# Probability scaling on GpSimd, modulation products pinned behind each convolution, and three operations for the FFN norm's columns

## The chip, the cores and the metric

One core of a Trainium2 chip runs the program. Its engines are TensorE (PE, with its weight loads PEld), VectorE (DVE), ScalarE (ACT), GpSimd (POOL) and SyncE (SP), whose queue issues most DMAs. Each engine works through its own queue in order, and engines meet at semaphores. The metric is the device time of one execution in microseconds (us), lower is better.

## The reference

One layer of a streaming encoder over 1024 tokens of width 1024, all in fp32:

```
mod = silu(c) @ w_ada + b_ada;  sh_m, sc_m, g_m, sh_f, sc_f, g_f = split(mod, 6)
h = rmsnorm(x, norm_mix_w) * (1 + sc_m) + sh_m
z, xbc, dt, q, k, v = split(h @ w_in)
y_ssd = ssd_mixer(z, silu(causal_dwconv4(xbc) + b), dt)     # 8 heads x 64, state 128
y_att = softmax(q k / 8 + bias over own chunk and 8 before) @ v   # 8 heads x 64, chunks of 64
x = x + g_m * (concat(y_ssd, y_att) @ w_out)
h = rmsnorm(x, norm_ffn_w) * (1 + sc_f) + sh_f
x = x + g_f * (silu(g) * val) @ w_down,   g, val = split(causal_dwconv3(h @ w_up))
out = rmsnorm(x)
```

A modulation column is a product of 1024 weights with silu(c) for each of 128 channels; there are 48 of them, eight for each of the six vectors.

## The kernel before

Everything stays on one core. Matrix products split each fp32 operand into a high and a low part (`split`, lines 60 to 66) and run three matmuls (`mm3`, L56 to L58). The stages in order of time are: norm and the first projections; attention by four pairs of heads; eight convolution columns of the SSD mixer; the z projection; the SSD scan; the output projection; the FFN.

**Attention.** For a pair of heads and a row block of 128 queries, `attn_scores` (L296) makes scores in a PSUM tile `s` (two buffers of two banks). L318 on DVE adds the bias and takes the maximum, L321 on ACT takes the exponential and the sum, L323 the reciprocal, and L324 on DVE scales the probabilities `p` by it. `attn_pv` (L328) transposes them on PE (L350, L353), splits the result (ACT L65, DVE L66) and multiplies with v. There are 64 scalings, 32 of them 128x640, the others shorter. `p` has eight buffers. Projections of the later pairs run between the pairs. Their weights are split into high (ACT, L65) and low (POOL, L66, tile `wl`) parts, so do the convolutions' weights. POOL also writes two memsets into each bias tile (L377, L378).

**Convolution columns.** `conv_silu` (L407) loads weights (L128), splits them, runs 48 matmuls into an `s` tile, evicts with a scale on ACT (L412), adds three shifted taps on DVE (L414), and then does tanh on ACT (L419) and a product on DVE (L420) for each half. The `s` tile comes free with the third tap. The order is four columns for B and C (`bt`, `ct`), then four for x (`xst`), whose results are transposed on PE (L492).

**Modulation products.** `mod_col` (L111) loads 512 KB of weights into a tile and multiplies and sums it on DVE (L113) against `rowa`. Behind each of the eight convolutions, `mods` makes three: the mixer gate, the FFN scale and the FFN shift. Their tiles `mt` come from the pool `mtp` with three buffers. `mod_scale` (L168, L170) and `mod_shift` (L174) turn each column into the FFN norm's columns `affn` and `bffn`, which are first read by L805 and L807. The FFN gate's eight products come later, from the tile tag `rm` (L582).

**z projection.** The pool `mtp` is closed at L519, and `wzp`, with the z weights `wzh` and `wzl` (four buffers each) and `zt`, is opened on the same side at L524. Raw weights pass through `raws`, a ring of two. L62 on ACT writes the high part and L63 on DVE the low part; `z_tile` (L537) reads both.

**What sets the order.** The code is written in one program order, and a scheduler places each instruction in its engine's queue by a planned time: among ready instructions the earlier in program order goes first, so a product of a later convolution may stand ahead of an earlier convolution's taps, and matmuls of the convolutions are placed between those of the last pair. `tc.issue_after(i)` keeps the instructions of its block behind `i` on `i`'s engine; it adds no semaphore. A tile's memory comes free when its last reader is done.

Of the kernel before, what the change touches and what calls it, by code (L numbers as in the profile page):

```python
# [13 lines left out]
ALU = mybir.AluOpType  # L14
# [5 lines left out]
KT = D // P  # L20
# [25 lines left out]
def tile_block(ctx: ExitStack, tc: tile.TileContext, x, crep, pk, w_ada, w_first, w_ft, w_z,  # L46
               w_out, w_up, w_down, bias, fnw, out, dbg=None):
    nc = tc.nc
    V, A, G, T = nc.vector, nc.scalar, nc.gpsimd, nc.tensor
# [31 lines left out]
    modc = const.tile([P, 48], F32, name="modc")  # L81
# [25 lines left out]
    def raw_tile(n=1024):  # L107
        rawc[0] += 1
        return raws[:, rawc[0] % 2, 0:n]

    def mod_col(ft, t):  # L111
        nc.sync.dma_start(t, w_ada[ft])
        V.tensor_tensor_reduce(out=t, in0=t, in1=rowa, scale=1.0, scalar=0.0,  # L113
                               op0=ALU.mult, op1=ALU.add, accum_out=modc[:, ft:ft + 1])

    def row_of(cols, dst, psp, tag, bufs, ones, tmp):
        for hh in range(2):
# [45 lines left out]
    affn = const.tile([P, 8], F32, name="affn")  # L163
    bffn = const.tile([P, 8], F32, name="bffn")

    def mod_scale(dst, sc, nw, kt):
        t = stat()
        V.tensor_tensor(t, modc[:, sc + kt:sc + kt + 1], pkt[:, B_ADA + sc + kt:B_ADA + sc + kt + 1],  # L168
                        ALU.add)
        V.scalar_tensor_tensor(dst[:, kt:kt + 1], t, 1.0, pkt[:, nw + kt:nw + kt + 1],  # L170
                               op0=ALU.add, op1=ALU.mult)

    def mod_shift(dst, sh, kt):
        V.tensor_tensor(dst[:, kt:kt + 1], modc[:, sh + kt:sh + kt + 1],  # L174
                        pkt[:, B_ADA + sh + kt:B_ADA + sh + kt + 1], ALU.add)

    V.tensor_scalar(pkt[:, SCW:FCW], pkt[:, SCW:FCW], 0.5, None, op0=ALU.mult)
    V.tensor_scalar(pkt[:, SNW:SCW], pkt[:, SNW:SCW], 512.0 ** 0.5, None, op0=ALU.mult)
# [63 lines left out]
    for hh in range(2):  # L242
        accs = [ps0.tile([P, 512], F32, tag="acc0", bufs=6, name="acc0") for _ in range(6)]
        for kt in range(KT):
            if hh == 0:
# [4 lines left out]
                t = raw_tile(768)  # L250
# [12 lines left out]
            c = slice(hh * 512, hh * 512 + 512)  # L263
# [23 lines left out]
    def s_tile():  # L287
        return ps1.tile([P, 1024], F32, tag="s", bufs=2, name="s")

    def p_tile():  # L290
        return pp.tile([P, 640], F32, tag="p", name="p")

    def tp_tile():
        return ps1.tile([P, 512], F32, tag="tp", bufs=2, name="tp")

    def attn_scores(p, i, bt):  # L296
        d = qk[p]
        j0 = max(0, i - 4)
        n = (i - j0 + 1) * P
        off = (j0 - (i - 4)) * P  # L300
        parts = [(0, n)] if n <= 512 else [(0, 320), (320, 320)]
        st = [s_tile(), s_tile()]
        for h in range(2):
            for pi, (a, w) in enumerate(parts):
                for ti, kn in enumerate(("kh", "kl")):
                    T.matmul(st[h][:, 512 * pi:512 * pi + w], d["q"][h][:, i * P:(i + 1) * P],  # L306
                             d[kn][h][:, j0 * P + a:j0 * P + a + w], start=ti == 0, stop=ti == 1)
        res = []
        for h in range(2):
            pt_ = p_tile()  # L310
            nm, rs = stat(), stat()
            if len(parts) == 1:
                src, bsl, dst = st[h][:, 0:n], bt[h][:, off:off + n], pt_[:, 0:n]
            else:
                src = st[h].rearrange("p (a b) -> p a b", a=2)[:, :, 0:320]
                bsl = bt[h].rearrange("p (a b) -> p a b", a=2)
                dst = pt_.rearrange("p (a b) -> p a b", a=2)
            V.tensor_tensor_reduce(out=dst, in0=src, in1=bsl, scale=-1.0, scalar=3e38,  # L318
                                   op0=ALU.add, op1=ALU.min, accum_out=nm)
            pv_ = pt_[:, 0:n]  # L320
            A.activation(pv_, pv_, AF.Exp, scale=-1.0, bias=nm, accum_out=rs)  # L321
            rr = stat()
            V.reciprocal(rr, rs)  # L323
            V.tensor_scalar(pv_, pv_, rr, None, op0=ALU.mult)  # L324
            res.append(pt_)
        return res

# [79 lines left out]
    def conv_silu(ft, dst, th2):  # L407
        wh, wl = wu_pair(w_ft[ft], A, G)
        ps = s_tile()
        gemm_ft(wh, wl, [ps[:, 0:512], ps[:, 512:1024]], hts_h, hts_l)  # L410
        w = [pkt[:, SCW + 4 * ft + j:SCW + 4 * ft + j + 1] for j in range(4)]
        A.activation(dst, ps, AF.Identity, scale=w[3], bias=pkt[:, SCB + ft:SCB + ft + 1])  # L412
        for j in range(1, 4):
            V.scalar_tensor_tensor(dst[:, j:S], ps[:, 0:S - j], w[3 - j], dst[:, j:S],  # L414
                                   op0=ALU.mult, op1=ALU.add)
        for hh in range(2):
            c = slice(hh * 512, hh * 512 + 512)
            th = th2()
            A.activation(th, dst[:, c], AF.Tanh)  # L419
            V.scalar_tensor_tensor(dst[:, c], th, 1.0, dst[:, c], op0=ALU.add, op1=ALU.mult)  # L420

    part = lambda p, w: (lambda: gemm_part(p, w))
    attention(0)
# [13 lines left out]
    bt_ = [bcx.tile([P, S], F32, name=f"bt{g}") for g in range(2)]  # L437
    ct_ = [bcx.tile([P, S], F32, name=f"ct{g}") for g in range(2)]
# [31 lines left out]
    def mt_tile():  # L470
        return mtp.tile([P, D], F32, tag="mt", bufs=MTB, name="mt")

    def mods(kt):
        mod_col(G_M + kt, mt_tile())
        mod_col(SC_F + kt, mt_tile())
        mod_scale(affn, SC_F, NFFN, kt)
        mod_col(SH_F + kt, mt_tile())
        mod_shift(bffn, SH_F, kt)

    for g in range(2):  # L480
        conv_silu(4 + g, bt_[g], th512)
        mods(2 * g)
        conv_silu(6 + g, ct_[g], th512)
        mods(2 * g + 1)
    for ft in range(4):
        xt = bcp.tile([P, S], F32, tag="rm", bufs=2, name="xst")
        conv_silu(ft, xt, th512)
        mods(4 + ft)
        for hh in range(2):
            tps = tp_tile()  # L490
            for j in range(4):
                T.transpose(tps[:, j * P:(j + 1) * P], xt[:, (4 * hh + j) * P:(4 * hh + j + 1) * P],  # L492
                            ident)
            A.activation(xs[:, 4 * hh:4 * hh + 4, ft * P:(ft + 1) * P],
                         tps.rearrange("p (a b) -> p a b", a=4), AF.Copy)
    wop_ = []
    halves = [slice(0, 512), slice(512, 1024)]
    order = [4, 5, 6, 7, 0, 1, 2, 3]
# [347 lines left out]
    class Unit:  # L846
# [98 lines left out]
    for sts in ((0, 1), (2, 3)):  # L945
        h_raw(sts)
        c = slice(sts[0] * P, sts[-1] * P + P)
# [61 lines left out]
    sc, last_load, busy, queue = [0], [], {}, []  # L1009
# [219 lines left out]
    last = product("P2", W, tail=True)  # L1229
# [63 lines left out]
```

## Time and profile before

| | us |
|---|---|
| median of 3 runs (1269.13 to 1275.05) | 1270.45 |
| the profiled execution | 1271.27 |
| its span, first to last instruction | 1269.6 |
| PE busy | 1189.2 |
| DVE busy | 984.6 |
| ACT busy | 560.4 |
| POOL busy | 108.0 |

A group's row gives line, engine and operation, out<-in, shapes and count, then busy time and mean ns, then idle time before it with what ended it. A row in order of time gives the start in us from the span's start, the length, the instruction, and in brackets the idle time of its engine before it with its releaser. A wait's row gives who waited for whom, the total in us, how often, and the longest. The granted clock is TensorE's, as a share of full speed.

### The profile page before, as it was taken

What the parts mean: (1) busy time and instruction counts of PE and PEld (TensorE: products, weight loads), DVE (VectorE), ACT (ScalarE), POOL (GpSimd) and SP (SyncE); (2) the same over time, 40 slices, a digit from 0 to 9 for tenths busy, and PEclk for the clock granted to TensorE, in tenths of its full rate; (3) what the DMA queues carried; (4) which work ended last, traced back from release to release, by engine and by line L of the source; (5) the groups of instructions that cost most, each with busy time, mean ns of one, the idle gap of its engine ahead of it and who ended that gap; (6) DMA issues with size and microseconds to landing.
All of it is one profiled execution on the core that took longest, in us unless ns stands there. A gap on an engine that the chain in (4) does not pass through costs nothing.

```text
span 1269.6 us, 15525 instructions
## 1 busy us (share of the span) xinstructions
PE 1189.2 (94%) x5786; PEld 991.8 (78%) x5786; DVE 984.6 (78%) x1533; ACT 560.4 (44%) x917; POOL 108.0 (9%) x114
## 2 busy tenths in 40 slices
PE   5898999989979979999889999999999999999995
PEld 3686788778869868888668888888888888888884
DVE  7836666694698886764999988888988879856976
ACT  4525555573324453423744444443444445443443
POOL 1300011101220242220000000000000000000002
PEclk9998899999989989999999999999999999999998
DMA  8712111201564422112213322323322295834433
GB/s 331 258 29 65 38 51 54 62 17 34 183 226 140 166 83 67 54 55 90 69 67 124 119 80 90 110 100 124 119 81 89 79 321 208 303 110 143 158 124 132
DMA packets 57835, 150.85 MB, mean 119 GB/s; under 512 B 5793, under 2 KB 5921, under 8 KB 56353
## 3 DMA queue, kind: packets, MB, share of 16 engines
q1 hardware_dynamic: 50704, 125.49, 29.4%
q10 hardware_dynamic: 7056, 24.38, 4.8%
q8 instruction: 45, 0.74, 0.2%
q14 instruction: 30, 0.24, 0.1%
HBM read 116.56 MB, written 29.10 MB: 115 GB/s over the span
## 4 chain that ended last, share of the span: by engine, by line
PE 76%; DVE 14%; DMA 4%; ACT 3%; issue 2%; POOL 1%; SPq 0%; DVEq 0%; POOLq 0%; ACTq 0%
PE dn L57 5%; PE dn L56 5%; PE dn L58 5%; PE uY L56 5%; PE uY L58 5%; PE uY L57 5%; PE uZ L58 3%; PE uZ L56 3%; PE uZ L57 3%; PE uX L56 3%; PE uX L58 3%; PE uX L57 3%; PE acc L56 3%; PE acc L57 3%; PE acc L58 2%
## 5 line engine op out<-in xcount | busy, mean ns | idle before, releaser
L56 PE MATMUL dn<-w 128*128 128x512 f32 x308 | 111.9, 389 | 0.0
L57 PE MATMUL dn<-w 128*128 128x512 f32 x308 | 111.9, 389 | 0.0
L58 PE MATMUL dn<-w 128*128 128x512 f32 x308 | 103.3, 389 | 0.0
L65 ACT ACTIVATE w<-ya 128x1024 fp32r<-128x1024 f32 (+1 forms) x44 | 41.8, 950 | 95.6 <-PE uY L58 87.1
L764 POOL TENSOR_TENSOR st<-st,mhalf 128x1 f32<-128x1 f32 x16 | 12.4, 777 | 678.2 <-DVE st L763 678.2
L56 PEld LDWEIGHTS dn<-w 128*128 128x128 f32 x308 | 57.8, 188 | 12.1
L57 PEld LDWEIGHTS dn<-w 128*128 128x128 f32 x308 | 57.8, 188 | 12.0
L58 PEld LDWEIGHTS dn<-w 128*128 128x128 f32 x308 | 57.8, 188 | 11.9
L65 ACT ACTIVATE w<-xs 128x1024 fp32r<-128x1024 f32 (+1 forms) x44 | 41.8, 951 | 43.5 <-PE uY L58 37.5
L56 PE MATMUL s<-hth,wh 128*128 128x512 f32 x128 | 51.7, 404 | 8.8 <-DVE st L168 8.0
L66 DVE TENSOR_TENSOR pt<-tp,pt 128x512 fp32r<-128x512 f32 (+2 forms) x72 | 42.0, 595 | 17.7 <-ACT pt L65 17.2
L318 DVE CUSTOM_DVE_ANT_0 p<-s,bias 128x640 f32<-128x640 f32 (+4 forms) x64 | 40.8, 649 | 18.4 <-PE s L306 10.1
L321 ACT ACTIVATE p<-p,st 128x640 f32<-128x640 f32 (+4 forms) x64 | 44.1, 691 | 19.8 <-DVE st L318 18.7
L66 POOL TENSOR_TENSOR wl<-raws,wh 128x1024 fp32r<-128x1024 f32 x14 | 36.5, 2612 | 189.3 <-ACT wh L65 145.9
L906 DVE SCALAR_TENSOR_TENSOR a<-cv,pkt,a 128x1023 f32<-128x1023 f32 (+1 forms) x40 | 51.0, 1276 | 0.1
L57 PE MATMUL s<-htl,wh 128*128 128x512 f32 x128 | 51.0, 398 | 0.0
L58 PE MATMUL s<-hth,wl 128*128 128x512 f32 x128 | 50.9, 398 | 0.0
L66 DVE TENSOR_TENSOR w<-ya,w 128x1024 fp32r<-128x1024 f32 (+1 forms) x44 | 47.7, 1085 | 4.0 <-ACT w L65 4.0
L113 DVE CUSTOM_DVE_ANT_0 mt<-mt,rows 128x1024 f32<-128x1024 f32 x32 | 41.6, 1301 | 10.6 <-DMA mt<-in_w_ada_dram 10.6
L906 DVE SCALAR_TENSOR_TENSOR a<-cg,pkt,a 128x1023 f32<-128x1023 f32 (+1 forms) x40 | 49.6, 1276 | 0.0
L65 ACT ACTIVATE pt<-tp 128x512 fp32r<-128x512 f32 (+2 forms) x72 | 36.3, 523 | 28.8 <-PE tp L350 12.3
L66 DVE TENSOR_TENSOR w<-xs,w 128x1024 fp32r<-128x1024 f32 (+1 forms) x44 | 47.6, 1083 | 0.0
(407 smaller groups left out, 3607.6 us busy)
## 6 DMA issues: line engine op xcount, KB each, us to landing
mt<-in_w_ada_dram SPq DMA_DIRECT2D x32, 512.0 KB, 3.8
gz<-a ACTq DMA_DIRECT2D x10, 1024.0 KB, 5.3
adat<-in_w_ada_dram SPq DMA_DIRECT2D x16, 512.0 KB, 6.5
ya<-in_w_up_dram SPq DMA_DIRECT2D x10, 768.0 KB, 4.0
xs<-in_w_up_dram SPq DMA_DIRECT2D x10, 768.0 KB, 4.1
raws<-in_w_ft_dram SPq DMA_DIRECT2D x14, 512.0 KB, 3.5
gy<-a ACTq DMA_DIRECT2D x10, 512.0 KB, 2.6
qk<-in_x_dram SPq DMA_DIRECT2D x8, 512.0 KB, 6.7
```

The costliest lines, as they stand in the source:

```text
L56: T.matmul(ps, lh, rh, start=start, stop=False, skip_group_check=more)
L57: T.matmul(ps, lh, rl, start=False, stop=False, skip_group_check=more)
L58: T.matmul(ps, ll, rh, start=False, stop=stop, skip_group_check=more)
L65: i = A.activation(hi, src, AF.Copy) if ehi is A else ehi.tensor_copy(hi, src)
L66: return i, elo.tensor_tensor(lo, src, f32(hi), ALU.subtract)
L113: V.tensor_tensor_reduce(out=t, in0=t, in1=rowa, scale=1.0, scalar=0.0, op0=ALU.mult, op1=ALU.add, accum_out=modc[:, ft:ft + 1])
L318: V.tensor_tensor_reduce(out=dst, in0=src, in1=bsl, scale=-1.0, scalar=3e38, op0=ALU.add, op1=ALU.min, accum_out=nm)
L321: A.activation(pv_, pv_, AF.Exp, scale=-1.0, bias=nm, accum_out=rs)
L764: G.tensor_tensor(r, ms, mhalf[:, 0:1], ALU.pow)
L906: V.scalar_tensor_tensor(a[:, j:S], c[:, 0:S - j], w[2 - j], a[:, j:S], op0=ALU.mult, op1=ALU.add)
```

## The change

Three edits. L324 moves from DVE (`V`) to POOL (`G`). `conv_silu` returns its last DVE instruction, and the three products of `mods` are issued behind it on DVE; their loads are not held. The FFN norm's columns are made once, behind the last convolution, for all eight columns at once: two operations for `affn` and one for `bffn` in place of 24 single-column ones.

```
     def mod_col(ft, t, at=None):
         nc.sync.dma_start(t, w_ada[ft])
+        with tc.issue_after(at) if at else ExitStack():
             V.tensor_tensor_reduce(out=t, in0=t, in1=rowa, ...)
...
-    def mod_scale(dst, sc, nw, kt):
+    def mod_scale(dst, sc, nw, kt, n=1):        # mod_shift likewise; columns kt to kt + n
...
-            V.tensor_scalar(pv_, pv_, rr, None, op0=ALU.mult)
+            G.tensor_scalar(pv_, pv_, rr, None, op0=ALU.mult)
...
-            V.scalar_tensor_tensor(dst[:, c], th, 1.0, dst[:, c], op0=ALU.add, op1=ALU.mult)
+            last = V.scalar_tensor_tensor(dst[:, c], th, 1.0, dst[:, c], op0=ALU.add, op1=ALU.mult)
+        return last.ins
...
-    def mods(kt):
-        mod_col(G_M + kt, mt_tile())
-        mod_col(SC_F + kt, mt_tile())
-        mod_scale(affn, SC_F, NFFN, kt)
-        mod_col(SH_F + kt, mt_tile())
-        mod_shift(bffn, SH_F, kt)
+    def mods(kt, at):
+        for m in (G_M, SC_F, SH_F):
+            mod_col(m + kt, mt_tile(), at)
...
-        conv_silu(4 + g, bt_[g], th512)
-        mods(2 * g)
-        conv_silu(6 + g, ct_[g], th512)
-        mods(2 * g + 1)
+        mods(2 * g, conv_silu(4 + g, bt_[g], th512))
+        mods(2 * g + 1, conv_silu(6 + g, ct_[g], th512))
...
-        conv_silu(ft, xt, th512)
-        mods(4 + ft)
+        mods(4 + ft, conv_silu(ft, xt, th512))
...
+    mod_scale(affn, SC_F, NFFN, 0, KT)
+    mod_shift(bffn, SH_F, 0, KT)
```

More of the change, by code (lines that the diff above doesn't have):

```diff
@@ L109, in raw_tile, with mod_col @@
         return raws[:, rawc[0] % 2, 0:n]
-    def mod_col(ft, t):
+    def mod_col(ft, t, at=None):
         nc.sync.dma_start(t, w_ada[ft])
-        V.tensor_tensor_reduce(out=t, in0=t, in1=rowa, scale=1.0, scalar=0.0,
-                               op0=ALU.mult, op1=ALU.add, accum_out=modc[:, ft:ft + 1])
+        with tc.issue_after(at) if at else ExitStack():
+            V.tensor_tensor_reduce(out=t, in0=t, in1=rowa, scale=1.0, scalar=0.0,
+                                   op0=ALU.mult, op1=ALU.add, accum_out=modc[:, ft:ft + 1])
     def row_of(cols, dst, psp, tag, bufs, ones, tmp):
@@ L164, in tile_block, with mod_shift @@
     bffn = const.tile([P, 8], F32, name="bffn")
-    def mod_scale(dst, sc, nw, kt):
-        t = stat()
-        V.tensor_tensor(t, modc[:, sc + kt:sc + kt + 1], pkt[:, B_ADA + sc + kt:B_ADA + sc + kt + 1],
+    def mod_scale(dst, sc, nw, kt, n=1):
+        t = stat(n)
+        V.tensor_tensor(t, modc[:, sc + kt:sc + kt + n], pkt[:, B_ADA + sc + kt:B_ADA + sc + kt + n],
                         ALU.add)
-        V.scalar_tensor_tensor(dst[:, kt:kt + 1], t, 1.0, pkt[:, nw + kt:nw + kt + 1],
+        V.scalar_tensor_tensor(dst[:, kt:kt + n], t, 1.0, pkt[:, nw + kt:nw + kt + n],
                                op0=ALU.add, op1=ALU.mult)
-    def mod_shift(dst, sh, kt):
-        V.tensor_tensor(dst[:, kt:kt + 1], modc[:, sh + kt:sh + kt + 1],
-                        pkt[:, B_ADA + sh + kt:B_ADA + sh + kt + 1], ALU.add)
+    def mod_shift(dst, sh, kt, n=1):
+        V.tensor_tensor(dst[:, kt:kt + n], modc[:, sh + kt:sh + kt + n],
+                        pkt[:, B_ADA + sh + kt:B_ADA + sh + kt + n], ALU.add)
     V.tensor_scalar(pkt[:, SCW:FCW], pkt[:, SCW:FCW], 0.5, None, op0=ALU.mult)
```

## The prediction

> **What bounds the kernel now.** I read the page first, then busy time by stage, then the waits and the order of time around the two stages that the diff touches.
>
> ```profile
> span 1269.6 us, 15525 instructions
> PE 1189.2 (94%) x5786; PEld 991.8 (78%) x5786; DVE 984.6 (78%) x1533; ACT 560.4 (44%) x917; POOL 108.0 (9%) x114
> ```
>
> TensorE (PE) is the bound: busy for 94% of the span. A change can only win by removing time in which PE stands still or runs at a low clock, and lose by adding some. GpSimd (POOL) is 9% busy. The profiled execution took 1271.27 us, 1.67 above its span, and 0.82 above the median of the runs (1270.45). The busy times of the stages concerned follow; the columns are the stretch, its length, PE, PEld, DVE, ACT and POOL busy with their instructions, the granted clock, the DMA share and GB/s.
>
> ```profile
> 118.00:133.00 15.00, 12.32 (x72) 9.51 (x71) 14.88 (x45) 12.79 (x31) 0.00 (x0) 0.99 0.08 22
> 250.00:287.00 37.00, 32.56 (x198) 26.89 (x196) 34.21 (x101) 27.64 (x67) 3.02 (x3) 0.95 0.08 23
> 350.00:360.00 10.00, 3.31 (x8) 2.66 (x9) 10.00 (x15) 1.85 (x3) 2.92 (x1) 0.56 0.60 202
> 395.00:460.00 65.00, 60.56 (x454) 55.91 (x453) 52.10 (x94) 28.78 (x64) 12.31 (x8) 1.00 0.43 147
> ```
>
> VectorE (DVE) is full in two stretches of the attention (118 to 133 and 250 to 287), where PE idles 2.68 and 4.44 us. It is full again in the convolution stage, where PE has one large hole at 350. Its cause, and what it costs, in the waits of PE and in PE's instructions in order of time:
>
> ```profile
> PE s L56 <- DVE st L168: 8.0, 1, 8.0
> ```
> ```profile
> 356.69 0.77 PE L56 MATMUL s<-hth,wh 128*128 128x512 f32 x1 [7.96 <-DVE st L168]
> 357.26 0.63 PE L57 MATMUL s<-htl,wh 128*128 128x512 f32 x1
> 357.69 0.63 PE L58 MATMUL s<-hth,wl 128*128 128x512 f32 x1
> ...
> 361.50 0.40 PE L58 MATMUL s<-hth,wl 128*128 128x512 f32 x1
> 361.74 0.40 PE L56 MATMUL s<-hth,wh 128*128 128x512 f32 x1
> ```
>
> PE waits 7.96 us for a score bank, which the third tap (L414) of the fourth convolution frees. Then 11 matmuls run 0.43 apart instead of 0.23: 11 x 0.20 = 2.2 us. The hole costs 10.2 us. DVE was late because modulation products stood ahead of that tap:
>
> ```profile
> 333.41 1.22 DVE L113 CUSTOM_DVE_ANT_0 mt<-mt,rows 128x1024 f32<-128x1024 f32 x1 [1.94 <-DMA mt<-in_w_ada_dram]
> ...
> 340.14 2.89 DVE L113 CUSTOM_DVE_ANT_0 mt<-mt,rows 128x1024 f32<-128x1024 f32 x1 [0.44 <-DMA mt<-in_w_ada_dram]
> ...
> 354.13 1.21 DVE L113 CUSTOM_DVE_ANT_0 mt<-mt,rows 128x1024 f32<-128x1024 f32 x1
> ...
> 355.28 1.27 DVE L414 SCALAR_TENSOR_TENSOR ct<-s,pkt,ct 128x1021 f32<-128x1021 f32 x1
> ```
> ```profile
> 338.86 3.09 POOL L66 TENSOR_TENSOR wl<-raws,wh 128x1024 fp32r<-128x1024 f32 x1 [2.58 <-ACT wh L65]
> ```
>
> Nine products ran from 333.41 to 354.13. The one at 340.14 took 2.89 instead of 1.22, and began to move when the split on POOL ended (338.86 + 3.09 = 341.95): the two engines block one another when both read two SBUF operands.
>
> **The change, part by part.**
>
> *Scaling (L324) on POOL.* 64 instructions leave DVE; these are the ones in the two full stretches (DVE only), and the nearest rows for a price on POOL:
>
> ```profile
> 118.00:133.00 15.00, 4.45 (x9) 0.99 0.08 22
> 250.00:287.00 37.00, 9.47 (x20) 0.95 0.08 23
> ```
> ```profile
> L66 POOL TENSOR_TENSOR wl<-raws,wh x14: 2378/2398/3503, 54.3 to 371.1; 128x1024 fp32r<-128x1024 f32 x14
> ```
> ```profile
> L96 POOL TENSOR_SCALAR st<-st x16: 221/222/1162, 8.0 to 587.9; 128x1 f32<-128x1 f32 x16
> ```
> ```profile
> PE tp L353 <- DVE p L324: 0.2, 1, 0.2
> ```
>
> DVE gains 4.45 and 9.47 us there, about 0.48 per block. The price of one 128x640 scaling on POOL lies between 0.22 (the fixed cost of the 128x1 row) and 2.40 x 640/1024 = 1.50 (two operands). I take 0.9, the middle, since the operation is that of the first row and the size nearer the second. A block is then 0.4 us later. That is hidden: PE waited for L324 only once, 0.2 us, because the DVE queue itself delayed the scaling. PE cannot win more than it idles: 2.68 + 4.44 = 7.1 us. ACT, 12.79 of 15 busy in the first stretch, is the next limit (15 - 12.79 = 2.2 of the 2.68). The chain through ACT and the in-order queues will take part of the rest. I take half: **-3.5**, ends -7.1 and 0. Without that cover, see the second rival. On POOL's queue the scalings stand among six of the 2.40 us splits and the bias memsets.
>
> The Trainium skill speaks against this gain ("Perfetto Trace Analysis", Optimizing Scalar/DVE Operations): since GpSimd reads through VectorE's second port, moving work between the two might not help. The blocked product at 340.14 agrees where both read SBUF twice. In the attention, L318, L66 and L367 each read one operand from PSUM, so I do not apply it; by it the sum would be 3.5 higher.
>
> *Products pinned.* The three products of a convolution may no longer run before its last L420. Their DMAs are not pinned, but the three mt buffers come free only with the products, so the loads wait too. On SP's queue the loads of the z weights may stand behind them; the product of the seventh convolution frees these before the seam below, so I cost that at nothing. Two places decide.
>
> First, the hole at 350. The attention's last DVE operation is the first row here; the second is one of the small ones that the diff merges:
>
> ```profile
> 335.92 0.42 DVE L367 TENSOR_TENSOR ya<-pv,tl 64x256 f32<-64x256 f32 x1
> ...
> 338.40 0.15 DVE L174 TENSOR_TENSOR bffn<-modc,pkt 128x1 f32<-128x1 f32 x1
> ```
>
> It ends at 336.3, and PE could start the GEMM at 356.69 - 7.96 = 348.7. Rows in order of time overlap their neighbours by about 0.07, so a tap counts 1.2. DVE must do in between: the first convolution's L420 (2 x 0.6), three products (3 x 1.21), the second's L420 (1.2), three products (3.6, if their loads are in time), the third's L420 (1.2), three taps (3 x 1.2), one block by a split (1.7 as at 340.14): 16.1, so 352.4. If the third three also come first, 356.0, nearly as now; if the second three are late, 348.8. I take 352.4: the hole shrinks from 8.0 to 3.7, and half the slow matmuls stay (1.1): 10.2 - 4.8 = **-5.4**, ends -10.2 and 0.
>
> The Trainium skill ("TensorE: Matmul & The Clock Gate", What's actually happening) lets the clock fall to half after about 3.4 us without work and for as long again; the 4.6 us from 356.69 fit it roughly. By it a gap of 3.7 us keeps the full penalty, and the sum would be 1.1 higher.
>
> Second, the seam to the z projection. The pool wzp is opened where the pool mtp was, so the z weights' low parts (wzl) lie on the mt tiles and must wait for the last three products. In the profile before these are early:
>
> ```profile
> 388.13 1.22 DVE L113 CUSTOM_DVE_ANT_0 mt<-mt,rows 128x1024 f32<-128x1024 f32 x1
> ...
> 390.68 1.30 DVE L63 SCALAR_TENSOR_TENSOR wzl<-raws,wzh 128x520 fp32r<-128x520 f32 x2
> ...
> 393.93 1.29 DVE L420 SCALAR_TENSOR_TENSOR xst<-th,xst 128x512 f32<-128x512 f32 x2 [0.76 <-ACT th L419]
> ```
> ```profile
> 393.27 1.16 ACT L419 ACTIVATE th<-xst 128x512 f32<-128x512 f32 x2 [2.36 <-DVE xst L414]
> ...
> 394.86 1.19 ACT L412 ACTIVATE xst<-s,pkt 128x1024 f32<-128x1024 f32 x1
> ```
> ```profile
> 394.15 0.41 PE L56 MATMUL zps<-wzh,hth 128*128 128x260 f32 x2
> ```
>
> The last product ran at 388.13, wzl followed at 390.68, and z began at 394.15, the moment the last convolution's GEMM ended. After the change the last three products stand behind that convolution's L420. From the end of its GEMM: 1.19 (L412) + 3 x 1.2 (L414) + 0.6 (tanh) + 2 x 0.6 (L420) + 3 x 1.21 (products) + 0.65 (wzl) = 10.9 us before PE can go on. PE has the transposes of two x tiles meanwhile, 4 x 0.44:
>
> ```profile
> 397.43 0.44 PE tp L492 x4
> ```
>
> So 10.9 - 1.8 = 9.1 us of new idling, and 2.2 of slow clock as at 356.69: **+11.3**. Ends: +10.1 if two products free enough, +15.5 if PE also waits for the third weight part, whose raw buffer comes free only with the first wzl (2.9 landing, 0.6, 0.65):
>
> ```profile
> raws<-in_w_z_dram SPq DMA_DIRECT2D x8, 260.0 KB, 2.9
> ```
>
> *What lies behind.* The work of that convolution no longer runs beside z, so DVE is freer from 395 to 460, where PE idles 65 - 60.56 = 4.4. I take **-2**, ends -4.4 and 0.
>
> *Norm columns in three operations instead of 24.* 21 small DVE operations go, of 0.15 us (338.40) at most: 3 us. Their readers come at 592, so nothing waits: 0 on the path by itself.
>
> Sum: -3.5 - 5.4 + 11.3 - 2 = +0.4 on 1271.27, and 0.82 below for the median: **1271 us**. All best ends give 1270.5 - 7.1 - 10.2 + 10.1 - 4.4 = 1259; all worst, 1270.5 + 15.5 = 1286.
>
> **Rivals.** *The pin wins outright.* The seam does not open, because the scheduler lets the z weights start on buffers that are free, and the hole goes: 1270.5 - 3.5 - 10.2 = 1257; or only the attention gives all it can, 1270.5 - 7.1 - 10.2 + 11.3 - 2 = 1262. For it: z's first matmul needs only the high part. Against: the order 388.13, 390.68.
>
> *Scalings queue behind splits (slower).* POOL runs in order, and a split of 2.40 us waits for ACT, which waits for PE. If the scalings of a block stand behind each of the six splits in the attention and PE has nothing else, 6 x 2.4 = 14.4 in place of -3.5: 1289. It decides from 1277 on, that is from two and a half splits. Against: PE has projection matmuls to fill with.
>
> *The pin does not clear the first hole (slower).* Nine products are allowed before the tap as now, if loads are early: 1271 + 5.4 + 2 = 1278.
>
> **How the numbers follow.** 0.5% (6.4 us) is about what a measurement of this kernel can tell from no change. Forecast 0.37 (within 0.5%); pin wins 0.25 (faster); queueing 0.18 and the uncleared hole 0.20 (slower). So faster 0.25, same 0.37, slower 0.38. The range 1259 to 1287 reaches from the best ends to near the queueing case; the forecast's own is 1264 to 1277.
>
> **What would show it.** Right: DVE under 12 of 15 in the first stretch with POOL 5 to 10 busy; the wait at 350 under 5 us; a new PE hole of 8 to 11 us before the first zps matmul, released by wzl. Wrong: a PE wait on POOL p L324 of several us, no hole before zps, or a PE wait of 8 us still at the sixth convolution.

## The result, and the profile after

The changed kernel takes 1276.28 us (median of 20 runs, 1273.11 to 1279.09), the kernel before 1269.45 (20 runs, 1266.0 to 1275.05). The ratio is 1.0049, with a 95% interval of 1.0038 to 1.0060: 0.5% slower, some 6.2 us. The forecast was 1271, within 1264 to 1277, and 1259 to 1287 over all its cases. The profiled execution took 1276.49 us, 1.69 above its span; that of before took 1271.27.

The head of the page of the changed kernel, and its group of scalings (busy us, mean ns of one, idle time before it):

```profile
span 1274.8 us, 15617 instructions
...
PE 1187.0 (93%) x5786; PEld 992.2 (78%) x5786; DVE 960.0 (75%) x1448; ACT 560.8 (44%) x917; POOL 199.0 (16%) x178
...
L325 POOL TENSOR_SCALAR p<-p,st 128x640 f32<-128x640 f32 (+4 forms) x64 | 94.1, 1486 | 30.1 <-DVE st L324 26.3
```

VectorE lost 85 instructions (1533 to 1448) and 24.6 us of work, GpSimd gained 91.0 us of work. In the attention, by stretch (columns as in the prediction):

```profile
118.00:133.00 15.00, 12.92 (x65) 10.46 (x65) 9.27 (x28) 8.80 (x21) 14.85 (x11) 0.89 0.14 46
...
250.00:287.00 37.00, 34.81 (x210) 30.39 (x209) 22.05 (x66) 21.70 (x52) 25.20 (x17) 0.94 0.00 1
```

VectorE was full there before; now GpSimd is the full engine of the first stretch, 14.85 of 15. TensorE idles 2.1 and 2.2 us instead of 2.7 and 4.4. Its waits later on (total us, times, longest):

```profile
PE s L56 <- DVE ct L415: 7.5, 1, 7.5
PE tp L488 <- DVE xst L421: 6.5, 1, 6.5
...
PE zps L57 <- DVE wzl L63: 3.1, 1, 3.1
...
PE uY L56 <- DVE cg L882: 3.1, 1, 3.1
```

The first is the old hole, hardly shorter than before (8.0). The next two are the new hole at the seam to z. The last is at the start of the FFN, where the same wait was 1.4 us before, and which the diff does not touch.

To see where time goes over the whole kernel, five instants are read from each trace. Two of the rows of the changed kernel (shortest, median, longest ns, then first and last start) are:

```profile
L368 DVE TENSOR_TENSOR ya<-pv,tl x32: 398/417/419, 117.1 to 327.5; 64x256 f32<-64x256 f32 x32
...
L58 PE MATMUL zps<-wzh,htl x64: 278/281/420, 400.5 to 447.1; 128*128 128x260 f32 x64
```

They are the first and the last attention output (117.1, 327.5), the last z matmul into a `zps` tile (447.1; those into `s` tiles end some 7 us later in both kernels), and, read in the same way, the first matmul of the FFN (uX, 614.6) and the first of its second part (dn, 1051.1). The stretches between them, in us, for all kernels of this study; the letters are those of the experiments below:

| kernel | to first output | attention | convolutions and z | z to FFN | FFN, first part | rest | median, ratio (95% interval) |
|---|---|---|---|---|---|---|---|
| before | 120.0 | 215.9 | 109.3 | 167.3 | 433.1 | 224.0 | 1269.45 |
| changed | 117.1 | 210.4 | 119.6 | 167.5 | 436.5 | 223.7 | 1276.28, 1.0049 (1.0038 to 1.0060) |
| A scaling alone | 117.7 | 209.5 | 110.7 | 168.4 | 434.8 | 223.6 | 1265.16, 0.9960 (0.9943 to 0.9977) |
| B pin alone | 117.9 | 215.6 | 121.0 | 166.6 | 434.9 | 223.7 | 1282.03, 1.0099 (1.0080 to 1.0118) |
| C columns alone | 117.9 | 217.0 | 110.1 | 169.3 | 434.8 | 223.6 | 1274.60, 1.0038 (1.0023 to 1.0052) |
| D pin and columns | 116.4 | 216.5 | 122.5 | 168.3 | 433.2 | 223.6 | 1282.55, 1.0109 (1.0089 to 1.0130) |
| E last three free | 117.8 | 207.5 | 117.3 | 167.4 | 436.4 | 223.7 | 1272.22, 1.0026 (1.0014 to 1.0039) |
| F tiles apart | 118.0 | 207.4 | 105.3 | 170.8 | 434.7 | 223.7 | 1262.36, 0.9948 (0.9930 to 0.9966) |
| G A, tiles apart | 120.7 | 207.8 | 110.2 | 169.1 | 434.7 | 223.7 | 1266.79, 0.9969 (0.9954 to 0.9984) |
| H A, behind the tap | 120.8 | 207.9 | 111.3 | 168.3 | 437.3 | 223.7 | 1269.42, 0.9997 (0.9984 to 1.0010) |
| I F, behind the tap | 119.2 | 207.4 | 103.4 | 172.3 | 434.8 | 223.6 | 1260.24, 0.9917 (0.9895 to 0.9938) |
| J two-tensor scaling | 120.4 | 209.4 | 120.5 | 167.9 | 434.7 | 223.7 | 1277.02, 1.0062 (1.0044 to 1.0081) |
| K I, six early | 126.6 | 208.7 | 101.5 | 169.6 | 433.1 | 223.7 | 1267.93, 0.9988 (0.9977 to 0.9999) |
| L I, six in the attention | 118.9 | 213.1 | 101.8 | 172.9 | 437.5 | 223.6 | 1267.90, 0.9989 (0.9978 to 1.0001) |

Each line is one profiled execution. The first column needs care: no kernel but K and L moves work into it other than the first few scalings, and yet without K it takes 116.4 to 120.8 us. The granted clock up to 118 us is 0.94 in four of the profiled executions (before, G, H and J), and they are those with 120 and more; in the others, K aside, it is 0.96 to 0.99. So differences of up to 3 us in this column go with the clock of the start. That clock does not follow the scaling (0.99 in A, 0.94 in G and H, which scale in the same place); whether the single execution sets it, one trace of each kernel cannot show. From before to the changed kernel: -2.9 here, -5.5 in the attention, +10.3 in the convolutions and z, +0.2, +3.4 in the FFN, -0.3: +5.2, the difference of the spans.

### The profile page after: what moved, and what is told of

Its sections match the earlier page's. It is cut to its first block, busy times and chain, and to the rows that moved or that the text cites. A ratio compares the mean times of both kernels' runs of the same rounds, so it can differ in the third digit from the quotient of the medians.

```text
span 1274.8 us, 15617 instructions
## 1 busy us (share of the span) xinstructions
PE 1187.0 (93%) x5786; PEld 992.2 (78%) x5786; DVE 960.0 (75%) x1448; ACT 560.8 (44%) x917; POOL 199.0 (16%) x178
## 4 chain that ended last, share of the span: by engine, by line
PE 79%; DVE 11%; ACT 4%; DMA 3%; issue 2%; POOL 1%; SPq 0%; DVEq 0%; POOLq 0%; ACTq 0%
PE dn L57 5%; PE dn L56 5%; PE dn L58 5%; PE uY L56 5%; PE uY L58 5%; PE uY L57 5%; PE uZ L56 3%; PE uZ L58 3%; PE uZ L57 3%; PE uX L56 3%; PE uX L57 3%; PE uX L58 3%; PE acc L56 3%; PE acc L57 3%; PE acc L58 3%; PE s L56 2%
## 5 line engine op out<-in xcount | busy, mean ns | idle before, releaser
L325 POOL TENSOR_SCALAR p<-p,st 128x640 f32<-128x640 f32 (+4 forms) x64 | 94.1, 1486 | 30.1 <-DVE st L324 26.3
L322 ACT ACTIVATE p<-p,st 128x640 f32<-128x640 f32 (+4 forms) x64 | 44.1, 690 | 13.1 <-DVE st L319 12.9
```

What stands on the lines that cost most here:

```text
L325: G.tensor_scalar(pv_, pv_, rr, None, op0=ALU.mult)
```

## The experiments

The theory was that the scaling gains, the pin loses at the seam, and the columns are free. The rivals were that a change of order far behind makes the loss, or that GpSimd's queue takes back the gain.

### A to D: the parts alone

A (`e1_scale`), on the kernel before:

```diff
-            V.tensor_scalar(pv_, pv_, rr, None, op0=ALU.mult)
+            G.tensor_scalar(pv_, pv_, rr, None, op0=ALU.mult)
```

> The kernel before with the scaling of the probabilities on GpSimd and nothing else; products unpinned, norm columns as before. Theory (the attention's gain is the scaling's, the loss is the pin's): the last evicted attention output on VectorE comes at about 328 us as in the changed kernel (before 335.9), x1's GEMM starts some 8 us earlier, no 6.5 + 3.1 us wait opens at the transposes of x and the z GEMM, and the time is about 8 us under the kernel before, 1261 to 1264 us. Rival A (the gain is given back at the first convolutions, because GpSimd's splits block the products as they were before the pin too): within 3 us of before. Rival B (the 3.4 us lost at the start of the FFN come from an order that the scaling moves): the wait of uY for cg shows 3 us instead of 1.4, and the time is near 1265.

B (`e2_pin`), the pin alone, with the norm columns one by one as before:

```diff
-        mods(2 * g)
+        mods(2 * g, conv_silu(4 + g, bt_[g], th512))
...
```

> The kernel before with the three products pinned behind each convolution and nothing else. Theory: the attention ends where it did (335.9 us on VectorE), the first hole stays at 7 to 8 us, and the seam opens as in the changed kernel: waits of 6.5 us of the transposes of x and of 3 us of the z GEMM for the low half of its weights. The time is 1277 to 1284 us. Rival A (the pin costs nothing by itself and only the shifted attention made the seam): within 2 us of 1269.5, no wait over 2 us at the seam. Rival B (the 3.4 us at the start of the FFN are the pin's, by the order of VectorE's instructions behind it): uY's wait for cg shows 3 us here.

C (`e3_merge`), the columns alone:

```diff
-        mod_scale(affn, SC_F, NFFN, kt)
-        mod_shift(bffn, SH_F, kt)
...
+    mod_scale(affn, SC_F, NFFN, 0, KT)
+    mod_shift(bffn, SH_F, 0, KT)
```

> The kernel before with the FFN norm's columns in three operations and nothing else. Theory: the columns are off the path, so that 1268 to 1271 us come out, with every wait up to 600 us as before. Rival (the merged columns make cg later and are the cause of the 3.4 us at the start of the FFN): uY's wait for cg grows from 1.4 to about 3 us, and the time is 1272 to 1274 us.

D (`e4_pin_merge`) is the changed kernel with the scaling back on VectorE:

```diff
-            G.tensor_scalar(pv_, pv_, rr, None, op0=ALU.mult)
+            V.tensor_scalar(pv_, pv_, rr, None, op0=ALU.mult)
```

> The changed kernel with the scaling back on VectorE. Theory (effects add): the scaling's gain of about 8 us is gone and the pin's loss stays, so that 1281 to 1286 us come out. Rival A (the queue of GpSimd costs what it gains): the time is that of the changed kernel, 1275 to 1278. Rival B (scaling on GpSimd was itself the loss): faster than the changed kernel, 1268 to 1272.

Measured: A is 0.4% faster than before, B 1.0% slower, C 0.4% slower, D 1.1% slower. Waits of TensorE in A, then in B, then one in C:

```profile
PE s L56 <- DVE st L168: 8.1, 1, 8.1
...
PE uY L56 <- DVE cg L884: 3.0, 1, 3.0
```
```profile
PE tp L491 <- DVE xst L421: 7.8, 1, 7.8
PE s L56 <- DVE ct L415: 7.6, 1, 7.6
...
PE zps L57 <- DVE wzl L63: 3.1, 1, 3.1
```
```profile
PE s L56 <- DVE zs L553: 2.2, 1, 2.2
```

The seam is the pin's: with it, convolutions and z take 119.6 to 122.5 us (changed, B, D), without it 109.3 to 110.7 (before, A, C), and B has both waits of the changed kernel though nothing else was done. The attention's gain is the scaling's: 215.6 to 217.0 us without it, 207.4 to 210.4 with it (L, which puts other work there, aside). B and D came out within the ranges of the theory. A is 1 us above its range, where its rival B put it, and shows that rival's sign, 3.0 us of uY's wait: its FFN takes 1.7 us longer than before, so a part of the gain is lost there. C was expected at no change and lost 4.8 us (0.38% of 1269.5), near what its rival said, and uY's wait is 3.0 there too. But this wait cannot be the cause: in A and C the wait just ahead of it (uZ for its weights) fell from 3.0 to 1.5, so that the two together are 4.5 against 4.4 before. The granted clock accounts for it: over the first 57 us of the FFN it is 0.94 in A and in C and 0.97 before, 0.03 x 57 = 1.7 us. The rest of C's loss is in no one place: against before, +1.1 in the attention, +0.8 in the convolutions and z (with 3.1 us of waits for `zs` in z, 0.3 before), +2.0 between z and the FFN, and -2.1 in the first column. The effects do not add: B and C sum to 17 us and D, which does both, loses 14.

### E to G: what makes the seam

E (`e5_last_free`), the changed kernel with the last three products free:

```diff
-        mods(4 + ft, conv_silu(ft, xt, th512))
+        at = conv_silu(ft, xt, th512)
+        mods(4 + ft, at if ft < 3 else None)
```

> The changed kernel with the three products of the last convolution not pinned. Theory (the seam is the low z weights waiting for memory that the last three products hold, and for their place behind that convolution's last operation): the wait of the z GEMM for the low weights (3.1 us) and the wait of the transposes ahead of it (6.5 us) go, the first hole stays at 7 to 8 us, and the time is 9 to 12 us under the changed kernel, 1264 to 1268 us. Rival (any pinned product moves the seam, since VectorE is simply late by the work that was pinned): the waits shrink by less than half and the time is 1272 to 1276.

F (`e6_mt_apart`), the changed kernel with the pool of the mt tiles kept open until the pool of the z weights closes, so that they share no bytes:

```diff
-    es_m.close()
...
     es_t.close()
+    es_m.close()
```

> The changed kernel with the modulation rows' tiles in memory of their own, so that the z weights share no bytes with them; the pins stay. Theory (the shared memory makes the wait, the pin only makes it late): the seam closes as with the last three products unpinned, 1264 to 1268 us. Rival (the place in VectorE's queue makes it, memory or not): the transposes still wait 4 us or more, and the time is within 3 us of the changed kernel.

G (`e10_free_apart`) is A with F's edit, so nothing is pinned.

> The kernel with the scaling on GpSimd alone (1265.2 us), with the modulation rows' tiles in memory of their own; nothing pinned. It tells what the pin does where the memory no longer makes it wait (against 1262.4 us with the pin, the merged columns and the same memory). Theory (the memory is the whole gain: the z GEMM can start before the last convolutions and fills TensorE): 1259 to 1264 us, the first hole stays at about 8 us, the first z matmul stands before 370 us. Rival (the pin helps once the memory is apart, because the products no longer take VectorE ahead of the taps): 1265 us or more.

Measured: E is 1272.2, where the rival put it, not 1264 to 1268. Its waits between 360 and 400 us:

```profile
PE s L56 <- DVE affn L171: 5.5, 1, 5.5
PE zps L56 <- ACT wzh L62: 1.9, 1, 1.9
```

The hole did not close: 7.4 us are left of 10.8. VectorE's rows in E, from the third pinned product of the convolution before to the split of the low z weights, and then the row with which TensorE goes on:

```profile
380.79 1.22 DVE L114 CUSTOM_DVE_ANT_0 mt<-mt,rows 128x1024 f32<-128x1024 f32 x1
...
383.32 1.23 DVE L114 CUSTOM_DVE_ANT_0 mt<-mt,rows 128x1024 f32<-128x1024 f32 x1 [1.31 <-DMA mt<-in_w_ada_dram]
...
389.51 1.22 DVE L114 CUSTOM_DVE_ANT_0 mt<-mt,rows 128x1024 f32<-128x1024 f32 x1
...
390.65 1.28 DVE L415 SCALAR_TENSOR_TENSOR xst<-s,pkt,xst 128x1021 f32<-128x1021 f32 x1
...
392.00 1.30 DVE L63 SCALAR_TENSOR_TENSOR wzl<-raws,wzh 128x520 fp32r<-128x520 f32 x2
```
```profile
392.08 0.56 PE L56 MATMUL s<-wzh,hth 128*128 128x260 f32 x1 [5.54 <-DVE affn L171]
```

The freed products are late all the same. There are three buffers, and the pinned products of the convolution before hold them until 382: the next load lands at 383.3, and VectorE stands idle for it. Four products follow, the freed ones among them, and now they stand between the taps of the last convolution (the third at 390.65). TensorE resumes at 392.08 with a z matmul that needs no low weights but a score bank, and that bank comes free with this third tap (390.65 + 1.28 = 391.93; the view names a small operation that ends a little later). Only behind the tap come the low weights, on the same bytes; their first matmul follows at 392.75. So the pin reaches one convolution further than the products that it holds, through their buffers. In F the z weights lie elsewhere, and the scheduler places the first split of the low ones early:

```profile
352.68 0.69 DVE L63 SCALAR_TENSOR_TENSOR wzl<-raws,wzh 128x520 fp32r<-128x520 f32 x1
```

and z starts before the convolutions have ended:

```profile
L56 PE MATMUL zps<-wzh,hth x64: 279/284/687, 359.4 to 430.5; 128*128 128x260 f32 x64
```

The waits at the seam are gone and the stage takes 105.3 us instead of 119.6. F is 1262.4, faster than the kernel before by 0.5%, with the pins in it and 1.6 us below the range of its theory: the shared memory makes the wait, as that theory says. G starts z at 362.5, as expected, but is 1266.8, on its rival's side: separate memory alone is worth nothing without the pins, 110.2 us in the stage against 110.7 in A. Without the pin the seam had no hole to close. G also has the columns unmerged, so G against F is not the pin alone, and their intervals meet.

### H and I: what makes the first hole

H (`e9_behind_tap`) is A with six products pinned behind the third tap of the fourth convolution, all others free:

```diff
...
-        mods(2 * g)
...
-        conv_silu(6 + g, ct_[g], th512)
-        mods(2 * g + 1)
+        if g == 0:
+            mods(0)
+        tap = conv_silu(6 + g, ct_[g], th512)
+        mods(2 * g + 1, tap if g else None)
+        if g == 1:
+            mods(2, tap)
```

> The kernel with the scaling on GpSimd alone (1265.2 us), and in it the six products of the third and fourth convolution pinned behind the third tap of the fourth, all others free. In that kernel five products and a blocked small operation stand on VectorE between 336 and 346 us ahead of the tap that frees the score bank. Theory (that queue makes the 8.1 us hole): the hole shrinks to 0 to 3 us, VectorE gets later by as much further on, so that part of it comes back before the z GEMM, and the time is 1257 to 1263. Rival (VectorE is the bound of the whole stage, 78.7 of 90 us busy): the wait only moves to a later place, and the time is within 2 us of 1265.

I (`c1_hole`) is F with nine products pinned there:

```diff
...
-        mods(2 * g, conv_silu(4 + g, bt_[g], th512))
-        mods(2 * g + 1, conv_silu(6 + g, ct_[g], th512))
+        last = conv_silu(4 + g, bt_[g], th512)[0]
+        if g == 0:
+            mods(0, last)
+        tap = conv_silu(6 + g, ct_[g], th512)[1]
+    for kt in (1, 2, 3):
+        mods(kt, tap)
```

> The changed kernel with the tiles in memory of their own (1262.4 us), and the nine products of the second to fourth convolution pinned behind the third tap of the fourth instead of behind their own convolution. Four of the seven products that stood ahead of that tap no longer do. Theory (the queue of VectorE makes the first hole, and the z GEMM, which may start early here, covers what comes later): the wait of 7.5 us falls under 2, and the time is 1251 to 1257 us. Rival (VectorE is the bound of this stage, 84 of 90 us busy, and what is moved behind the tap stalls the next convolutions): the time is 1260 to 1264 us.

Measured: the hole is made by the products, as the theory says. It falls to 2.7 us in H, and in I to 0.8, with a new wait in its place:

```profile
PE zps L57 <- DVE wzl L63: 5.6, 2, 3.9
...
PE s L56 <- DVE ct L415: 0.8, 1, 0.8
```

But the gain is not kept. H takes 111.3 us in the stage (A: 110.7) and is 4 us slower than A, above what its theory and its rival gave; in the traces its first column is 3.1 us longer and its FFN 2.5, its attention 1.6 shorter. I gains 1.9 us in the stage and loses 1.5 between z and the FFN. Its windows show VectorE full, as it is before (third busy number):

```profile
340.00:350.00 10.00, 9.52 (x42) 7.93 (x43) 10.00 (x13) 3.84 (x5) 3.41 (x1) 1.00 0.53 185
350.00:360.00 10.00, 6.08 (x26) 5.20 (x25) 10.00 (x12) 3.30 (x4) 2.56 (x1) 0.83 0.66 204
```

I came out where its rival put it: the work that is moved behind the tap stands ahead of the next thing that TensorE needs, the low z weights. I is the fastest kernel of the study, 1260.2 us, 0.8% under the kernel before. Its interval and F's meet, so whether it beats F is not settled.

### J: the price of a scaling on GpSimd

J (`e7_scale_tt`), on the changed kernel:

```diff
-            G.tensor_scalar(pv_, pv_, rr, None, op0=ALU.mult)
+            G.tensor_tensor(pv_, pv_, rr.to_broadcast([P, n]), ALU.mult)
```

> The changed kernel with the scaling on GpSimd as a product of two tensors, the second the reciprocal broadcast along the row, in place of the one-tensor form. It tells what sets the price of the form. Theory (a one-tensor operation with a scalar per row is dearer per element on GpSimd than a two-tensor one): a 128x640 scaling takes 1.3 to 1.5 us instead of 1.89, GpSimd is busy about 11 of the 15 us from 118 instead of 14.85, and the time falls by 0 to 3 us. Rival (a broadcast operand costs as much): 1.9 us or more for one, and the time is within 2 us of the changed kernel or above it.

The groups of the 128x640 scaling: before (VectorE), changed, and J, and for the first two the VectorE operation of the same size beside it:

```profile
L318 DVE CUSTOM_DVE_ANT_0 p<-s,bias 128x640 f32<-128x640 f32 x32 | 25.8, 811 | 8.6 <-PE s L306 8.6
L324 DVE TENSOR_SCALAR p<-p,st 128x640 f32<-128x640 f32 x32 | 17.0, 548 | 0.2
```
```profile
L325 POOL TENSOR_SCALAR p<-p,st 128x640 f32<-128x640 f32 x32 | 59.8, 1886 | 1.3 <-DVE st L324 1.0
...
L319 DVE CUSTOM_DVE_ANT_0 p<-s,bias 128x640 f32<-128x640 f32 x32 | 25.7, 816 | 6.4 <-PE s L307 5.9 <-PE tp L351 0.2
```
```profile
L325 POOL TENSOR_TENSOR p<-p,st 128x640 f32<-128x640 f32 x32 | 39.6, 1254 | 7.9 <-DVE st L324 6.7 <-PE tp L354 0.5
```

On GpSimd the one-tensor form takes 1.886 us, 3.4 times VectorE's 0.548, and the two-tensor form 1.254. The theory on the price held, a little under its range (1.3 to 1.5); that on the time did not. J's attention takes 209.4 us against 210.4, and its whole 1277.0 against 1276.3. A third off the price of every scaling moved nothing that can be measured, though GpSimd is busy for 11.0 instead of 14.85 us of the stretch from 118: TensorE hardly waits for a scaling in either kernel.

### K and L: less work for VectorE

K (`c2_early`) is I with six of the convolutions' 24 products done right behind the projections of the later pairs, on the raw weight tiles:

```diff
             evac_qkv(p, which, hh, outs[hh], tmp, tps)
+        if early[0] < KT:
+            mod_col(SC_F + early[0], raw_tile())
+            early[0] += 1
...
-        for m in (G_M, SC_F, SH_F):
+        for m in (G_M, SC_F, SH_F) if kt >= early[0] else (G_M, SH_F):
```

> The kernel that clears the first hole with the tiles apart (1260.2 us), and six of its modulation products (SC_F) taken to the first projections, onto the raw weight tiles, where VectorE is busy about 40% of the time (25 of 58 us from 60 to 118). In the kernel it starts from VectorE is busy for the whole of 330 to 360 us, the z GEMM waits 3.9 us for its low weights there, and 14.6 instead of 10 us lie between the last z matmul and the output projection. Theory (VectorE's work bounds this stage once no memory and no order does): 7 us of VectorE's work less give 3 to 6 us, 1254 to 1257 us. Rival (the six products delay the first projections or their loads as much, or the gain is given back between z and the output projection): 1259 to 1263.

L (`c3_in_attn`) pins these six behind the latest attention output, `mod_col(SC_F + early[0], raw_tile(), last_ya[0])`.

> The kernel with six products taken forward (1267.9 us), and these six pinned behind an attention output of the pair before, so that they fall into the attention (VectorE 64 of 117 us busy from 133 to 250) and not into the first projections, which they made 7.4 us longer (first attention output at 126.6 instead of 119.2 us). Theory (the projections' delay was the only price, and the relief from the last attention output to the output projection, 1.9 + 2.2 us, stays): first output back at 118 to 121 us, 1253 to 1258 us. Rival (in the attention they hold the raw weight tiles or block GpSimd's scalings, and the attention gets longer by 3 us or more than 207.4 us): 1260 to 1264.

Both rivals named what happened, but K and L are 5 and 4 us above even their ranges (1259 to 1263, 1260 to 1264). Convolutions and z fell to 101.5 and 101.8 us, the lowest of all, and in K another 2.7 us went between z and the FFN. But K's first attention output came 7.4 us later (126.6), and L's attention took 5.7 us longer (213.1). VectorE's mean share in those stages (25 of 58 us, 64 of 117) was not room. In L, TensorE's waits for VectorE to clear a score tile in the attention are 5.4 us instead of 2.6. In K the granted clock from 60 to 118 us is 0.85 instead of 0.95; whether the products or their loads, which take turns with other weights in the raw tiles, make K late was not separated.

## Why the prediction was right, and where it was wrong

The time came out 5 us above the forecast and inside its own range of 1264 to 1277, but at its very end and nearer to the 1278 of the rival in which the hole is not cleared. Of the signs it named, VectorE's load in the first stretch (9.27 of 15) and the new hole (10.8 us, in three pieces) came; GpSimd's 5 to 10 us there (14.85) and the wait under 5 us (7.5) did not. That the time lies in the range is in good part luck, as the steps show.

- **The scalings' price** was taken as 0.9 us, between 0.22 and 1.50; it is 1.886. The upper bound, by elements from a two-operand row, failed because on GpSimd the one-tensor form is the dearer one (J: 1.254 for two). It did not matter: the transposes' weight loads waited 0.5 us in all for the scalings, by the view of L325.
- **The attention's gain** of 3.5 was mis-sized: 5.5 us in the changed kernel, and 5 to 10 over the kernels with and without the scaling, past the end of 7.1. The step "PE cannot win more than it idles" failed. In the changed kernel TensorE idles only 1.6 us less between the first and the last output (11.1 to 9.5), and the clock is no better (0.89, 0.99 and 0.93 in the first 15, the next 117 and the next 37 us from the first output, against 0.93, 0.98 and 0.95). Eight matmuls fewer start in the stretch (1144 for 1152), so part of the gain is work that falls outside it; how much of the other 3.9 us that is, is not resolved. In other kernels the granted clock counts too, as the prediction itself held at the holes: in these rows of before and of F, TensorE's idle time from 133 to 250 us is no smaller after, and the clock is 0.99 instead of 0.97; from 250 to 287 it is 1.00 instead of 0.95.

```profile
133.00:250.00 117.00, 113.02 (x630) 96.37 (x630) 72.86 (x195) 59.87 (x135) 13.33 (x13) 0.97 0.18 50
```
```profile
133.00:250.00 117.00, 112.27 (x656) 96.49 (x655) 64.54 (x176) 67.62 (x153) 63.42 (x48) 0.99 0.19 54
...
250.00:287.00 37.00, 34.59 (x211) 29.25 (x210) 23.37 (x68) 23.31 (x55) 24.71 (x18) 1.00 0.00 1
```

  By these, 0.02 x 117 + 0.05 x 37 = 4.2 of F's 8.5 us are clock, and 1.8 less idle time in the three stretches (11.1 to 9.3); F too has eight matmuls fewer there, and the rest is not resolved.
- **The shared port.** The Trainium skill ("Perfetto Trace Analysis", Optimizing Scalar/DVE Operations) says that moving work between VectorE and GpSimd might not help, since they share a read port, which a two-port operation of VectorE locks. The trace shows no such loss in the attention: VectorE's 128x640 operation beside the scalings, which reads one operand from PSUM, kept its length (811 and 816 ns). Where both engines read two operands from SBUF there is one, as the next point shows.
- **The first hole** was to shrink from 8.0 to 3.7, with a gain of 5.4; it is 7.5, and the gain is nothing. The third rival, that the pin does not clear it, was right here. TensorE was ready 8.2 us earlier (340.5 instead of 348.7) and VectorE 8.4, and the prediction's list of VectorE's work in between was too short. In the changed kernel:

```profile
327.53 0.42 DVE L368 TENSOR_TENSOR ya<-pv,tl 64x256 f32<-64x256 f32 x1 [4.25 <-ACT tl L367]
...
330.68 3.42 DVE L114 CUSTOM_DVE_ANT_0 mt<-mt,rows 128x1024 f32<-128x1024 f32 x1
...
341.67 2.71 DVE L421 SCALAR_TENSOR_TENSOR bt<-th,bt 128x512 f32<-128x512 f32 x1
...
346.59 1.27 DVE L415 SCALAR_TENSOR_TENSOR ct<-s,pkt,ct 128x1021 f32<-128x1021 f32 x1
...
393.04 1.22 DVE L114 CUSTOM_DVE_ANT_0 mt<-mt,rows 128x1024 f32<-128x1024 f32 x1
...
399.34 1.30 DVE L63 SCALAR_TENSOR_TENSOR wzl<-raws,wzh 128x520 fp32r<-128x520 f32 x2
```

  From the last attention output to the end of the tap it is 19.9 us and not 16.1: seven products instead of six (1.2), and two blocks by splits on GpSimd, which run from 330.62 and 341.49 (3.42 for 1.22 and 2.71 for 0.68, so 4.2), instead of one of 1.7. That a product of a pinned group still goes ahead of the tap of a later convolution was the flaw of the edit; I, which pins them behind that tap, has 0.8.
- **The seam** was forecast at +11.3, 9.1 of it idle. Idle are 6.5 + 1.2 + 3.1 = 10.8, and the slow clock behind it (0.54 from 400 to 405) costs 0.46 x 5 = 2.3: 13.1, above the forecast and inside its ends of 10.1 and 15.5. The rows at 393.04 and 399.34 are the order of pinned products ahead of the low z weights that the step foresaw, but only the last 3.1 us end with those weights; the first 6.5 end with the last convolution's own product (xst, L421), with nothing of z ready to run ahead of the transposes, and 1.2 with the high weights. The loads on SP's queue, costed at nothing, are indeed late (the second pair of raw z weights is issued at 400.06, behind twelve mt loads that take 33 us), but TensorE, slow from 400 to 405, reaches those weights without a further wait:

```profile
366.55 33.23 SPq L112 DMA_DIRECT2D mt<-in_w_ada_dram  x12
400.06 0.94 SPq L530 DMA_DIRECT2D raws<-in_w_z_dram  x2
```

  The first rival, that the pin wins outright, did not come; without the shared memory, in F, the seam closes.
- **What lies behind** was to give 2 us back, and did, inside z: from z's start to its last `zps` matmul TensorE idles 2.5 us before, and 0.1 in the changed kernel once the low weights are there. With it convolutions and z were to grow by 11.3 - 5.4 - 2 = 3.9 us, and grew by 10.3. The stretch from z to the FFN did not change (167.3, 167.5).
- **The start of the FFN** stood in no step: +3.4. The VectorE rows there, of before and then of the changed kernel, and each with the TensorE row that waits:

```profile
647.56 0.69 DVE L884 TENSOR_TENSOR cg<-cv,uY 128x512 f32<-128x512 f32 x1
648.15 1.22 DVE L66 TENSOR_TENSOR w<-xs,w 128x1024 fp32r<-128x1024 f32 x1
```
```profile
648.39 0.47 PE L56 MATMUL uY<-t3h,w 128*128 128x512 f32 x1 [1.36 <-DVE cg L884]
```
```profile
649.71 1.21 DVE L66 TENSOR_TENSOR w<-xs,w 128x1024 fp32r<-128x1024 f32 x1
650.84 0.68 DVE L856 TENSOR_TENSOR ya<-ya 128x512 f32<-128x512 f32 x1
651.44 1.27 DVE L882 TENSOR_TENSOR cg<-cv,uY 128x512 f32<-128x512 f32 x2
```
```profile
652.26 0.47 PE L56 MATMUL uY<-t3h,w 128*128 128x512 f32 x1 [3.08 <-DVE cg L882]
```

  A split and a sum now stand ahead of the subtraction that frees TensorE's bank: 651.44 - 649.71 = 1.73 us, and the wait grew by 1.72. The granted clock from 27 to 57 us behind the first matmul of the FFN is 0.91 against 0.97, 0.06 x 30 = 1.8 us, which is the rest of the 3.4. This sum holds for all fourteen kernels: less TensorE's idle time and its loss by the granted clock in the first 57 us, the first part of the FFN takes 422.6 to 423.4 us in each. K shows the two terms apart: it idles there as long as the changed kernel (9.7 and 9.8 us), but at full clock, and takes 433.1. The order of VectorE's work goes along: the nine kernels with the first order need 433.1 to 434.8 us for this part, the five with the second (changed, B, E, H, L) 434.9 to 437.5. Nothing in the diff speaks of this place; the scheduler's planned times moved. What sets the clock there, and whether the order by itself is the cause, was not tried.
- **The columns** at 0 "on the path by itself": in C they cost 4.8 us, 1.7 of it clock in the FFN, with waits for `zs` in z that the columns' code does not touch. That a shift of planned times does it, as in the FFN, is argued and not shown. Together with the pin they cost nothing that can be told (B and D).

So the forecast's sum was near because errors cancelled. On the spans of these two executions it was +0.4, and +5.2 came: the start 2.9 better (with a granted clock of 0.99 instead of 0.94), the attention 2.0 better (-5.5 for -3.5), convolutions and z 6.4 worse (+10.3 for 3.9), z to FFN 0.2 worse, the FFN 3.4 worse and the rest 0.3 better.

The earlier a kernel is through with z, the longer is, as a tendency, its way from there to the FFN: 166.6 us in B, the second latest, and 172.3 in I, the earliest. VectorE is not full there (115.4 of 167.1 us before, 120.4 of 172.1 in I); TensorE idles 12.8 and 14.5 us. Why a part of a gain is lost there stays open.

## What to carry to other kernels

When work is pinned behind a stage, list what waits for that work: here it was not its result, which is read 200 us later, but its three buffers, and the next stage's tiles on the same bytes; with memory of its own the same pin no longer made a seam. Pin behind the instruction that frees the scarce thing (the tap that frees a bank), not behind the end of the step before it; that cleared the first hole, though little of it was kept here. And a move that leaves an engine's total as it was may only move the wait, as in I: look at the windows for the engine that becomes full, and expect part of any gain to come back where the order downstream is replanned.

## What was not expected of the hardware

On GpSimd a 128x640 scaling by a value per row takes 1.886 us, and the same product with the value broadcast as a second tensor 1.254. The Trainium skill ("GPSIMD Engine Reference", 4.1 Engine selection) has one-input operations at roughly line rate there and two-input ones about twice as slow as on VectorE; the measured order is the other way round, and the measurement decides.

The low clock does not need a gap of one fixed length. After 3.02 us of waiting in the kernel before, the matmuls ran slow from the first on; after 3.71 us in K they ran at full speed for the next 1.3 us, until 364.40; the 512-column matmuls behind that row take 0.63 us, as the slow ones of the kernel before do, against 0.39 at full speed:

```profile
637.88 0.78 PE L58 MATMUL uZ<-t1h,w 128*128 128x512 f32 x1 [3.02 <-DVE w L66]
638.46 0.63 PE L56 MATMUL uZ<-t1h,w 128*128 128x512 f32 x1
```
```profile
363.10 0.39 PE L57 MATMUL zps<-wzl,hth 128*128 128x260 f32 x1 [3.71 <-DVE wzl L63]
363.32 0.28 PE L58 MATMUL zps<-wzh,htl 128*128 128x260 f32 x1
...
364.40 0.71 PE L56 MATMUL s<-hth,wh 128*128 128x512 f32 x1
```

The Trainium skill ("TensorE: Matmul & The Clock Gate", What's actually happening) has a window of about 3.4 us that runs free of the program; the spread of these two agrees with a free-running window, though 3.02 us, less than that window, were already enough for one of them.
